# Stick-breaking attention: scores and values on the full array, tails in float32r, and one float32 group per head

## The chip, the core and the metric

The kernel runs on one core of a Trainium2 chip. The metric is the time of one execution in device microseconds; lower is better. Engine names as the profile has them: PE is TensorE (PEld its weight loads), ACT ScalarE, DVE VectorE, POOL GpSimd, SP SyncE, which issues the DMAs.

## What is computed

A decoder trunk of two layers on 256 positions of 1024 features, in float32. Each sub-layer is a norm, a modulation whose columns are products of the condition `c` with `mod_w`, a mixer or a SwiGLU, and a gated sum onto `x`. The change lies in the mixer of layer 0, which has eight gMLP heads and eight heads of stick-breaking attention:

```python
z = jnp.einsum('bqhd,bkhd->bhqk', qb, kb) * scale            # scores
before = s_pos < t_pos
log_1mb = jnp.where(before, -jax.nn.softplus(z), 0.0)
tail = lax.cumsum(log_1mb, axis=3, reverse=True) - log_1mb   # tails
w = jnp.where(before, jnp.exp(jax.nn.log_sigmoid(z) + tail), 0.0)
outs.append(jnp.einsum('bhqk,bkhd->bqhd', w.astype(v.dtype), v[:, :kv_len]))   # values
```

and around it

```python
proj = h @ w_in          # u, v of the gMLP heads; q, k, v of the attention
y_a = u * sv             # gMLP: v normed, mixed over positions ("gating")
x = x + g2[:, None, :] * (jnp.concatenate([y_a, y_b], -1) @ w_out)
```

## The kernel before

Activations are kept transposed: features on the 128 partitions, the 256 positions in the columns. A large product is made of three float32r products (`mm3`, L473): each operand is split into a rounded high half and the rest, and high x high, high x low and low x high are summed in PSUM. Weights come as 1 MB loads into four buffers (`raw`); ScalarE casts the high halves (`split_hi`, h_...), VectorE subtracts to get the low ones (`split_lo`, l_...), each 128x1024. A product of two float32 operands without a split needs no halves; its instruction runs as two passes.

Every instruction is placed by hand in one program order, and each engine keeps it. A planner, `Pace` (L36), estimates the end of every engine's work as the kernel is written out. `pump` (L453), called after blocks of products, runs what is due: splits, deferred evictions (`defer`, `run_deferred`) and the dots of the modulation columns (`mod_step`, L406). One dot is a VectorE instruction over 128x1024 (mw) that yields one eighth of a column vector; a load of mw brings two of them into one of two buffers, and the next load is issued behind the second dot. `mod_need` (L432) runs what is still missing at once. The columns (0, 7), mod07, scale the input of the SwiGLU behind the mixer: `enter` (L481) asks for them, and VectorE's updates of `xT` and the new `hh` come after that.

`hybrid` (L774) runs the mixer. q and k go into the tiles qT and kT, two heads in one 128-row block, 64 rows each. Then a loop over i = 0 to 10 (L1006) staggers the eight heads:

- `scores(h)` (L901): three float32 products of 64x128 into one bank `z`. Deferred behind it is the softplus: Abs, Exp and Ln on ScalarE into `sp`, max and sum on VectorE, and a causal mask by GpSimd (`diag`, L897, 128x256).
- `tails(h)` (L923), two rounds later: `sp` times `negtri` (384 columns) and times `neg1` (128 columns) are added onto `z`, in float32. Deferred: ScalarE's exponential into `w`, and GpSimd's mask of `w`.
- `values(h)` (L939), one more round later: three float32 products of `w` with 64 columns of `vb` into one half of the partitions of a bank `py`. Deferred for each pair of heads: the split into yh and yl.
- `fill(n)` takes n steps of other work: the projections `pvb` (products of 512 columns) and `pu` (of 256). From i = 7 on, the output projection `pdh` takes that place.
- `gating(j)` (L968), twice: sixteen float32 products of 64 columns, `pg`. `gelu_u` (L990) loads ScalarE's gelu table, runs it, and loads the old table back.

Behind the loop come the rest of the output projection, from yh and yl and from the split gMLP result (ahya, alya), and its last unit (`down_last`, L617). The next layer part starts with `pe`, whose products read hh.

```python
            if 0 <= i - 2 < 8:
                tails(i - 2)
            if i in (5, 6):
                gating(i - 5)
            if 0 <= i - 3 < 8:
                values(i - 3)
```

Of the kernel before, what the change touches and what calls it, by code (L numbers as in the profile page):

```python
# [20 lines left out]
HD = 64  # L21
# [4 lines left out]
HALF = 8  # L26
# [62 lines left out]
def trunk(ctx: ExitStack, tc: tile.TileContext, x, c, mod_w, cols,  # L89
# [124 lines left out]
    def cp(out_, in_):  # L214
        fill_act([in_], [out_])
        nc.scalar.copy(out=out_, in_=in_)  # L216
        return clk.op("act", free(out_) * 0.833 + 92, [in_], [out_])
# [14 lines left out]
    def keep_if(t, pattern, cmp, mult=-1):  # L232

        nc.gpsimd.affine_select(out=t, in_=t, pattern=pattern, base=0, channel_multiplier=mult, compare_op=cmp,
                                fill=0.0)
        return clk.op("pool", free(t) * 1.0 + 110, [t], [t])
# [21 lines left out]
    nc.vector.memset(eps_t, EPS)  # L258
    mean_w = const.tile([P, P], F32, name="mean_w")
    nc.gpsimd.memset(mean_w, 1.0 / D)  # L260
    neg1 = const.tile([P, P], F32, name="neg1")
    nc.gpsimd.memset(neg1, -1.0)
    negtri = const.tile([P, P], F32, name="negtri")
    nc.gpsimd.memset(negtri, -1.0)

    keep_if(negtri, [[-1, P]], ALU.is_ge, 1)

    cond = const.tile([P, D], F32, name="cond")

# [170 lines left out]
    def defer(t, fn):  # L440
        i = len(deferred)
        while i and deferred[i - 1][0] > t:
            i -= 1
        deferred.insert(i, (t, fn))

    def run_deferred(force=False):
        while deferred and (force or deferred[0][0] <= clk.pe):
            if state["on"] and can_l() and q["l"] - q["take"] < LOW and lo_start() <= clk.dve + SLACK:
                split_lo()
            else:  # L450
                deferred.pop(0)[1]()
# [322 lines left out]
    def hybrid(nxt):  # L774
# [31 lines left out]
        def run(gen):  # L806
            for _ in gen:
                pass

        qT = new(mix, "qT", "qT", 1, (P, 4, S))  # L810
        kT = new(mix, "kT", "kT", 1, (P, 4, S))

        def first_qk():
            for j in range(2):
                u, col = unfold(ps0[0][j], r, f"q{j}")
                ts(qT[:, j, :], u, col[:, 0:1], HD ** -0.5, ALU.add, ALU.mult)
                u, col = unfold(ps0[1][j], r, f"k{j}")
                ts(kT[:, j, :], u, col[:, 0:1], None, ALU.add)

        defer(clk.pe + 4000, first_qk)  # L820
        psq = dbank("pq1")
# [2 lines left out]
                                  scale=HD ** -0.5))  # L824
        psk = dbank("pk1")
        run(proj_t(psk, 4))
        defer(clk.pe, lambda: cp(kT[:, 2:4, :], psk.rearrange("p (j s) -> p j s", j=2)))


        wsT = new(mix, "wsT", "wsT", 1, (P, 8, P))  # L830
# [59 lines left out]
        def fill(n):  # L890
            for _ in range(n):
                next(filler, None)
# [3 lines left out]

        def diag(t):  # L897
            tv = t[:, 0:256].rearrange("p (b t) -> p b t", b=2)
            keep_if(tv, [[0, 2], [1, P]], ALU.is_gt)

        def scores(h):  # L901
            z = gbank(f"z{h}")
            r0 = 64 * (h % 2)
            qs = qT[r0:r0 + 64, h // 2, :]
            ks = kT[r0:r0 + 64, h // 2, :]
            for i, (s, t) in enumerate(((0, 0), (1, 1), (0, 1))):
                mm(z[:, i * P:(i + 1) * P], ks[:, s * P:(s + 1) * P], qs[:, t * P:(t + 1) * P], i == 0, True)
            zz = z[:, 0:384]
            sp = new(work, "e1", f"sp{h}", 4, (P, 384))

            def chain():
                act(sp, zz, AF.Abs)
                act(sp, sp, AF.Exp, scale=-1.0)
                defer(act(sp, sp, AF.Ln, bias=1.0), softplus)

            def softplus():
                stt(sp, zz, 0.0, sp, ALU.max, ALU.add)
                diag(sp)
                zs[h] = (z, sp)

            defer(clk.pe, chain)

        def tails(h):  # L923
            while h not in zs:
                run_deferred(True)
            z, sp = zs.pop(h)
            zz = z[:, 0:384]
            mm(zz, negtri, sp, False, False)
            mm(z[:, 256:384], neg1, sp[:, 128:256], False, True)
            w = new(work, "ah", f"w{h}", 4, (P, 384), F32R).bitcast(F32)  # L930

            def weights():
                act(w, zz, AF.Exp)
                diag(w)
                ws[h] = w

            defer(clk.pe, weights)

        def values(h):  # L939
            while h not in ws:  # L940
                run_deferred(True)
            w = ws.pop(h)
            hp, r0 = h // 2, 64 * (h % 2)
            if h % 2 == 0:
                pys[hp] = (dbank if hp < 2 else gbank)(f"py{hp}")
            py = pys[hp]
            for i, (s, t, src) in enumerate(((0, 0, 0), (0, 1, 2), (1, 1, 1))):
                mm(py[r0:r0 + 64, t * P:(t + 1) * P], vb[:, s, h * HD:(h + 1) * HD], w[:, src * P:(src + 1) * P],
                   i == 0, i == 2)
            if h % 2 == 1:  # L950
                if hp % 2 == 0:
                    ah = new(work, "ah", f"yh{hp}", 4, (P, 2, S), F32R)
                    al = new(work, "al", f"yl{hp}", 4, (P, 2, S), F32R)
                    yb.append((ah, al))
                ah, al = yb[-1]

                def keep():
                    defer(cp(ah[:, hp % 2, :], py[:, 0:S]), keep_lo)

                def keep_lo():  # L960
                    tt(al[:, hp % 2, :], py[:, 0:S], ah[:, hp % 2, :].bitcast(F32), ALU.subtract)

                defer(clk.pe, keep)

# [3 lines left out]
        def gating(j):  # L968
            pg = dbank(f"pg{j}")
            for i in range(2):  # L970
                hp = 2 * j + i
                for e in range(2):
                    for n in range(2):
                        h = 2 * hp + e
                        mm(pg[64 * e:64 * e + 64, i * S + n * P:i * S + (n + 1) * P], v[:, n, h * HD:(h + 1) * HD],
                           wsT[:, h, :], i == 0 and n == 0, True)

            def keep():
                for i in range(2):
                    hp = 2 * j + i  # L980
                    bb = bs_bc[:, hp, :].unsqueeze(1).to_broadcast([P, 2, P])
                    stt(yas[j][:, i, :].rearrange("p (n t) -> p n t", n=2),
                        pg[:, i * S:(i + 1) * S].rearrange("p (n t) -> p n t", n=2),
                        cols_a[:, VG + hp:VG + hp + 1], bb, ALU.mult, ALU.add)

            defer(clk.pe, keep)
# [16 lines left out]

        banks = []
        out_b = None
        for i in range(11):  # L1006
            if i < 8:
                scores(i)
            fill((3, 3, 2, 1, 2, 1, 2, 1, 1, 1, 1)[i])
            if 0 <= i - 2 < 8:  # L1010
                tails(i - 2)
            if i == 9:
                defer(clk.pe, gelu_u)
            if i in (5, 6):
                gating(i - 5)
            if i >= 7:
                if i == 7:
                    run(filler)
                    run_deferred(True)
                    banks += [dbank(f"pdh_{b}") for b in range(4)]  # L1020
                    out_b = down_steps(banks, lambda: yb[0], True)
                for _ in range(4):
                    next(out_b, None)
            if 0 <= i - 3 < 8:
                values(i - 3)
        run(out_b)
        run_deferred(True)
        down(banks, *yb[1], False)
# [360 lines left out]
```

## Time and profile before

| | |
|---|---|
| Median of three runs | 990.71 us (990.59 to 990.95) |
| The profiled execution | 990.8 us, of which the span of instructions is 989.1 |
| PE busy | 975.3 us, 99% of the span |
| PEld busy | 959.7 us, 97% |
| DVE busy | 764.0 us, 77% |
| ACT busy | 491.8 us, 50% |
| POOL busy | 24.7 us, 3% |
| Chain that ended last, by engine | PE 94%, DVE 4%, ACT 1%, DMA 1% |
| Mean granted TensorE clock | 0.996 of full speed |

Busy times of engines overlap, and a busy PE need not be at its peak. The chain is followed back from the last instruction: at each step to what released it, or to the instruction before it on its engine. The attention stage runs from about 250.7 us to 303.2 us of the span.

### The profile page before, as it was taken

To read this page: it belongs to the slowest core of one execution; us is meant where nothing else is said; L and a number is where in the kernel's file an instruction comes from. 1 tells how busy PE (TensorE), PEld (TensorE's weight loads), DVE (VectorE), ACT (ScalarE), POOL (GpSimd) and SP (SyncE) were. 2 spreads that over 40 slices of the span, in tenths; PEclk is the share of its full clock that TensorE was granted. 3 is DMA by queue.
4 is the path that set the end of the run, shared out by engine and by line. 5 is a ranking of instruction groups with operands and counts; after the bars stand their busy time and mean duration, and the time that the engine had idled before them with its cause. 6 is when DMAs were issued, how large, how long until landed. Compare 5 with 4: busy or idle time off the path is not lost.

```text
span 989.1 us, 18921 instructions
## 1 busy us (share of the span) xinstructions
PE 975.3 (99%) x7958; PEld 959.7 (97%) x7958; DVE 764.0 (77%) x1118; ACT 491.8 (50%) x691; POOL 24.7 (3%) x34
## 2 busy tenths in 40 slices
PE   6999999999999999999999999999999999999997
PEld 6999999999789999999999999999999999999997
DVE  6988877889878987777789777778998798744432
ACT  3566344365756754443466434444644574444333
POOL 4000000000220000000000000000000000000000
PEclk8999999999999999999999999999999999999999
DMA  9988997965877388897865988888269729665401
GB/s 354 331 312 286 330 335 279 332 213 188 315 253 256 130 294 298 304 324 282 294 222 164 329 320 315 294 319 298 80 210 338 254 89 322 229 214 171 170 2 43
DMA packets 144213, 249.59 MB, mean 252 GB/s; under 512 B 4216, under 2 KB 107520, under 8 KB 144128
## 3 DMA queue, kind: packets, MB, share of 16 engines
q1 hardware_dynamic: 144128, 248.39, 70.9%
q8 instruction: 62, 1.02, 0.4%
q14 instruction: 23, 0.19, 0.1%
HBM read 247.32 MB, written 1.05 MB: 251 GB/s over the span
## 4 chain that ended last, share of the span: by engine, by line
PE 94%; DVE 4%; ACT 1%; DMA 1%; issue 0%; DVEq 0%; SPq 0%; ACTq 0%
PE pf L139 44%; PE pd L139 25%; PE pc L139 3%; PE pe L139 3%; PE pcb L139 2%; PE pdc L139 2%; DVE mws L199 1%; PE pdh L139 1%; PE z L139 1%; PE pu L139 1%; PE pvb L139 1%; PE peh L139 1%; PE pec L139 1%; PE pv L139 1%; PE ps L139 1%; PE py L139 1%
## 5 line engine op out<-in xcount | busy, mean ns | idle before, releaser
L139 PE MATMUL pd<-ah,l_d 128*128 128x256 f32 x704 | 198.2, 281 | 0.0
L139 PE MATMUL pd<-al,h_d 128*128 128x256 f32 x704 | 198.0, 281 | 0.0
L139 PE MATMUL pd<-ah,h_d 128*128 128x256 f32 x704 | 198.0, 281 | 0.0
L139 PE MATMUL pf<-hh,h_u 128*128 128x256 f32 x608 | 172.0, 283 | 0.0
L139 PE MATMUL pf<-hl,h_u 128*128 128x256 f32 x608 | 171.2, 282 | 0.0
L139 PE MATMUL pf<-hh,l_g 128*128 128x256 f32 x608 | 171.1, 281 | 0.0
L139 PE MATMUL pf<-hl,h_g 128*128 128x256 f32 x608 | 171.0, 281 | 0.0
L139 PE MATMUL pf<-hh,h_g 128*128 128x256 f32 x608 | 171.0, 281 | 0.0
L139 PE MATMUL pf<-hh,l_u 128*128 128x256 f32 x608 | 170.9, 281 | 0.0
L199 DVE CUSTOM_DVE_ANT_0 mw<-mw,cond,cols_sb 128x1024 f32<-128x1024 f32 x128 | 163.7, 1306 | 3.4 <-DMA mw<-in_mod_w_dram 3.4
L216 ACT CAST h_d<-w_d 128x1024 fp32r<-128x1024 f32 x88 | 88.4, 1047 | 125.4 <-PE pf L139 98.8
L176 DVE TENSOR_TENSOR l_d<-w_d,h_d 128x1024 fp32r<-128x1024 f32 x88 | 104.5, 1221 | 55.9 <-ACT h_d L216 55.9
L216 ACT CAST h_g<-w_g 128x1024 fp32r<-128x1024 f32 x82 | 85.9, 1048 | 114.8 <-issue 78.8
L139 PEld LDWEIGHTS pd<-al,h_d 128*128 128x128 f32 x704 | 132.6, 188 | 0.0
L139 PEld LDWEIGHTS pd<-ah,h_d 128*128 128x128 f32 x704 | 132.5, 188 | 0.0
L139 PEld LDWEIGHTS pd<-ah,l_d 128*128 128x128 f32 x704 | 132.5, 188 | 0.0
L176 DVE TENSOR_TENSOR l_g<-w_g,h_g 128x1024 fp32r<-128x1024 f32 x82 | 100.0, 1220 | 40.1 <-ACT h_g L216 40.0
L139 PEld LDWEIGHTS pf<-hh,l_u 128*128 128x128 f32 x608 | 115.1, 189 | 0.0
L139 PEld LDWEIGHTS pf<-hl,h_u 128*128 128x128 f32 x608 | 114.9, 189 | 0.0
L139 PEld LDWEIGHTS pf<-hh,l_g 128*128 128x128 f32 x608 | 114.8, 189 | 0.0
L139 PEld LDWEIGHTS pf<-hh,h_g 128*128 128x128 f32 x608 | 114.8, 189 | 0.0
L139 PEld LDWEIGHTS pf<-hh,h_u 128*128 128x128 f32 x608 | 114.8, 189 | 0.0
(302 smaller groups left out, 1927.1 us busy)
## 6 DMA issues: line engine op xcount, KB each, us to landing
mw<-in_mod_w_dram SPq DMA_DIRECT2D x64, 1024.0 KB, 7.0
w_d<-in_ffn_w_down_dram SPq DMA_DIRECT2D x44, 1024.0 KB, 6.4
w_g<-in_ffn_w_gate_dram SPq DMA_DIRECT2D x41, 1024.0 KB, 6.2
w_u<-in_ffn_w_up_dram SPq DMA_DIRECT2D x41, 1024.0 KB, 5.0
mws<-in_mod_w_dram SPq DMA_DIRECT2D x14, 512.0 KB, 7.0
w_ho<-in_hy_w_out_dram SPq DMA_DIRECT2D x4, 1024.0 KB, 9.1
w_cc<-in_sc_w_in_dram SPq DMA_DIRECT2D x4, 1024.0 KB, 5.3
w_cx<-in_sc_w_in_dram SPq DMA_DIRECT2D x4, 1024.0 KB, 7.4
```

What stands on the lines that cost most here:

```text
L139: return nc.tensor.matmul(out=out_, lhsT=lhsT, rhs=rhs, start=start, stop=stop, skip_group_check=True)
L176: nc.vector.tensor_tensor(out=out_, in0=a, in1=b, op=op)
L199: nc.vector.tensor_tensor_reduce(out=src, in0=src, in1=cond, scale=scale, scalar=init, op0=ALU.mult, op1=ALU.add, accum_out=dst)
L216: nc.scalar.copy(out=out_, in_=in_)
```

## The change

Five things. The scores use all 128 rows: k is kept in two versions, in each of which the 64 rows of the other head of the pair are zero (memsets by GpSimd; the second version of the heads 4 to 7 and of the heads 0 to 3 lies in the tiles of `al`). The values use all 128 columns: the product takes both heads of a pair from `vb`, each head of the pair has a half of the bank's columns, and the half of the rows that belongs to it is read out, so the evictions into kT, yh and yl are done in two instructions of 64 partitions. The tails take float32r products of the softplus split into `sh` (ScalarE cast, behind the mask) and `sl` (VectorE subtraction); `negtri` and `neg1` become float32r. `w` takes the place of `sp`. And the loop is written in another order: a part of the fill, values, gating, scores, the rest of the fill, tails.

```diff
+        kT1 = [new(work, "al", f"kT1{k}", 4, (P, 2, S), F32R).bitcast(F32) for k in range(2)]
+        kTs = [[kT[:, 2 * k:2 * k + 2, :] for k in range(2)], kT1]
+        heads = [slice(64 * e, 64 * e + 64) for e in range(2)]
+        for e in range(2):
+            for k in range(2):
+                zeros = kTs[e][k][heads[1 - e]]
+                nc.gpsimd.memset(zeros, 0.0)
...
-            qs = qT[r0:r0 + 64, h // 2, :]
-            ks = kT[r0:r0 + 64, h // 2, :]
+            qs = qT[:, h // 2, :]
+            ks = kTs[h % 2][h // 4][:, h // 2 % 2, :]
...
-                diag(sp)
-                zs[h] = (z, sp)
+                defer(diag(sp), halves)
+
+            def halves():
+                sh = new(work, "sq", f"sh{h}", 2, (P, 384), F32R)
+
+                def rest():
+                    sl = new(work, "sl", f"sl{h}", 2, (P, 384), F32R)
+                    tt(sl, sp, sh.bitcast(F32), ALU.subtract)
+                    zs[h] = (z, sp, sh, sl)
+
+                defer(cp(sh, sp), rest)
...
-            mm(zz, negtri, sp, False, False)
-            mm(z[:, 256:384], neg1, sp[:, 128:256], False, True)
-            w = new(work, "ah", f"w{h}", 4, (P, 384), F32R).bitcast(F32)
+            for part in (sh, sl):
+                mm(zz, negtri, part, False, False)
+                mm(z[:, 256:384], neg1, part[:, 128:256], False, part is sl)
+            w = sp
...
-                mm(py[r0:r0 + 64, t * P:(t + 1) * P], vb[:, s, h * HD:(h + 1) * HD], w[:, src * P:(src + 1) * P],
+                mm(py[:, c0 + t * P:c0 + (t + 1) * P], vb[:, s, hp * P:(hp + 1) * P], w[:, src * P:(src + 1) * P],
...
+        def beside(n):
+            if out_b is None:
+                fill(n)
+            else:
+                for _ in range(3 * n):
+                    next(out_b, None)
+
         for i in range(11):
+            if i == 8:
+                run(filler)
+                run_deferred(True)
+                banks += [dbank(f"pdh_{b}") for b in range(4)]
+                out_b = down_steps(banks, lambda: yb[0], True)
+            beside((0, 0, 1, 1, 1, 1, 1, 1, 2, 2, 2)[i])
+            if 0 <= i - 3 < 8:
+                values(i - 3)
+            if i in (5, 6):
+                gating(i - 5)
             if i < 8:
                 scores(i)
-            fill((3, 3, 2, 1, 2, 1, 2, 1, 1, 1, 1)[i])
+            if i == 9:
+                defer(clk.pe, gelu_u)
+            beside((3, 3, 1, 1, 1, 1, 0, 0, 0, 0, 0)[i])
             if 0 <= i - 2 < 8:
                 tails(i - 2)
```

TensorE's row at i = 6, before:

```order
L139 MATMUL z_3086<-sp_3090,negtri 128x384
L139 MATMUL z_3086<-sp_3090,neg_102 128x128
L139 MATMUL pg_3240<-wsT,v 64x128 x8
L139 MATMUL py_3184<-w_3174,vb 64x128 x3
L139 MATMUL z_3252<-qT,kT 128x128 x3
L139 MATMUL pu_3193<-hh_2443,h_uu_1_3001 128x256
```

and in the changed kernel (twelve products `pu` stand ahead of the first row, and the tails of this head's predecessor ahead of those):

```order
L139 MATMUL pu_3183<-hh_2445,l_uu_1_3064 128x256
L139 MATMUL py_3205<-sp_3090,vb 128x128 x3
L139 MATMUL pg_3275<-wsT,v 64x128 x8
L139 MATMUL z_3284<-qT,kT 128x128 x3
L139 MATMUL z_3147<-sh_3201,negtri 128x384
L139 MATMUL z_3147<-sh_3201,neg_102 128x128
L139 MATMUL z_3147<-sl_3229,negtri 128x384
L139 MATMUL z_3147<-sl_3229,neg_102 128x128
L139 MATMUL pu_3183<-hh_2445,h_uu_1_3011 128x256
```

The tails moved from ahead of the values to behind the scores, and only a fill stands between the tails of a head and its values.

ScalarE's row at the last two heads (w6 and w7 are the exponentials before; in the changed kernel they are written onto sp6 and sp7), before:

```order
L211 ACTIVATE w6_3333<-z6_3188 128x384
L216 CAST h_ho1_1_3348<-w_ho1_3031 128x1024
L216 CAST yh2_3357<-py2_3327 128x256
L211 ACTIVATE w7_3361<-z7_3252 128x384
L226 ACT_TABLE_LOAD
L211 ACTIVATE uT_2836<-uT_2836 128x1024
L226 ACT_TABLE_LOAD
```

and in the changed kernel:

```order
L216 CAST yh2_3384<-py2_3324 64x256 x2
L211 ACTIVATE sp6_3288<-z6_3284 128x384
L216 CAST h_ho1_1_3403<-w_ho1_3072 128x1024
L226 ACT_TABLE_LOAD
L211 ACTIVATE uT_2844<-uT_2844 128x1024
L226 ACT_TABLE_LOAD
L211 ACTIVATE sp7_3332<-z7_3328 128x384
```

The exponential of the last head moved behind the gelu and its two table loads.

VectorE's row at the end of the mixer, from the last low half that both kernels have there to the first update of `xT`, before:

```order
L176 TENSOR_TENSOR l_g01_1_1_3545<-w_g01_1_3274,h_g01_1_1_3513 128x1024
L199 ISA mw072_3298,mod07_3282<-mw072_3298,cond_107,cols_sb_89 128x1024
L199 ISA mod07_3282 128x1
L199 ISA mw073_3352,mod07_3282<-mw073_3352,cond_107,cols_sb_89 128x1024
L199 ISA mod07_3282 128x1
L199 ISA mw073_3352,mod07_3282<-mw073_3352,cond_107,cols_sb_89 128x1024
L199 ISA mod07_3282 128x1
```

and in the changed kernel, where one dot of mw070 already stands ahead of the first row:

```order
L176 TENSOR_TENSOR l_g01_1_1_3596<-w_g01_1_3312,h_g01_1_1_3562 128x1024
L199 ISA mw070_3356,mod07_3580<-mw070_3356,cond_109,cols_sb_89 128x1024
L199 ISA mod07_3580 128x1
L199 ISA mw071_3418,mod07_3580<-mw071_3418,cond_109,cols_sb_89 128x1024
L199 ISA mod07_3580 128x1
L199 ISA mw071_3418,mod07_3580<-mw071_3418,cond_109,cols_sb_89 128x1024
L199 ISA mod07_3580 128x1
L176 TENSOR_TENSOR l_u01_1_1_3607<-w_u01_1_3455,h_u01_1_1_3594 128x1024
L199 ISA mw072_3601,mod07_3580<-mw072_3601,cond_109,cols_sb_89 128x1024
L199 ISA mod07_3580 128x1
L199 ISA mw072_3601,mod07_3580<-mw072_3601,cond_109,cols_sb_89 128x1024
L199 ISA mod07_3580 128x1
```

Two more dots, of mw073, follow. SyncE's row of loads at the same place, before:

```order
L391 DMA mw072_3298<-in_mod_w_dram 128x2x1024
L391 DMA mw073_3352<-in_mod_w_dram 128x2x1024
L301 DMA w_u01_1_3383<-in_ffn_w_up_dram 128x8x256
L301 DMA w_g01_2_3491<-in_ffn_w_gate_dram 128x8x256
L301 DMA w_u01_2_3511<-in_ffn_w_up_dram 128x8x256
L301 DMA w_d01_0_3547<-in_ffn_w_down_dram 128x2x1024
L391 DMA mw080_3550<-in_mod_w_dram 128x2x1024
```

and in the changed kernel:

```order
L393 DMA mw071_3418<-in_mod_w_dram 128x2x1024
L303 DMA w_u01_1_3455<-in_ffn_w_up_dram 128x8x256
L303 DMA w_g01_2_3526<-in_ffn_w_gate_dram 128x8x256
L303 DMA w_u01_2_3544<-in_ffn_w_up_dram 128x8x256
L303 DMA w_d01_0_3598<-in_ffn_w_down_dram 128x2x1024
L393 DMA mw072_3601<-in_mod_w_dram 128x2x1024
L393 DMA mw073_3605<-in_mod_w_dram 128x2x1024
```

The loads mw072 and mw073 moved from ahead of w_u01_1 to behind w_d01_0.

## Rows read from the trace of the kernel before

**Rows 1.** Waits of TensorE: waiting and releaser, us in total, times, longest.

```profile
PE ps L139 <- ACT hh L216: 4.6, 1, 4.6
```

**Rows 2.** Chain in order of time, the stage: start, us, engine, tile, line, instructions.

```profile
233.91 5.70 PE pk L139 x48
239.61 11.13 PE pv L139 x48
...
268.42 0.87 PE z L139 x4
...
302.39 0.80 PE py L139 x6
```

**Rows 3.** The same chain at the end of the mixer.

```profile
311.85 1.06 ACT h_g L216
...
314.16 1.26 DVE mw L199
```

**Rows 4.** Instructions in time, TensorE: start, us from first start to last end.

```profile
250.35 0.40 PE L139 MATMUL pv<-h_v,hl 128*128 128x512 f32 x1
250.67 0.93 PE L139 MATMUL z<-qT,kT 64*128 64x128 f32 x6
251.53 0.50 PE L139 MATMUL pvb<-h_vb,hh 128*128 128x512 f32 x1
251.87 0.39 PE L139 MATMUL pvb<-l_vb,hh 128*128 128x512 f32 x1
...
268.25 0.81 PE L139 MATMUL z<-sp,negtri 128*128 128x384 f32 x2
268.90 0.38 PE L139 MATMUL z<-sp,neg 128*128 128x128 f32 x2
269.21 0.87 PE L139 MATMUL py<-w,vb 128*64 128x128 f32 x6
...
320.32 0.28 PE L139 MATMUL pe<-hh,h_g 128*128 128x258 f32 x1
```

**Rows 5.** Instructions on tile z: count, ns least/median/most, first and last start.

```profile
L139 PE MATMUL z<-sp,neg x16: 271/274/275, 265.6 to 298.3; 128*128 128x128 f32 x16
```

**Rows 6.** Instructions in time, ScalarE.

```profile
269.32 0.49 ACT L211 ACTIVATE w<-z 128x384 f32<-128x384 f32 x1
...
295.74 1.04 ACT L216 CAST h_ho<-w_ho 128x1024 fp32r<-128x1024 f32 x1
...
299.43 1.28 ACT L226 ACT_TABLE_LOAD   x1
...
303.10 0.62 ACT L216 CAST ahya<-ya 128x512 fp32r<-128x512 f32 x1
```

**Rows 7.** Instructions in time, GpSimd; in brackets the idle time ahead.

```profile
269.10 1.39 POOL L234 TENSOR_SCALAR_AFFINE_SELECT sp<-sp 128x256 f32<-128x256 f32 x1 [2.04 <-DVE sp L187]
```

**Rows 8.** Instructions on tile sp, the masks: ns least/median/most.

```profile
L234 POOL TENSOR_SCALAR_AFFINE_SELECT sp<-sp x8: 406/837/1448, 259.6 to 290.4; 128x256 f32<-128x256 f32 x8
```

**Rows 9.** Instructions in time, VectorE.

```profile
268.95 1.27 DVE L199 CUSTOM_DVE_ANT_0 mw<-mw,cond,cols_sb 128x1024 f32<-128x1024 f32 x1
...
305.49 1.23 DVE L176 TENSOR_TENSOR l_g<-w_g,h_g 128x1024 fp32r<-128x1024 f32 x1
306.63 1.22 DVE L176 TENSOR_TENSOR l_u<-w_u,h_u 128x1024 fp32r<-128x1024 f32 x1
...
317.87 0.17 DVE L176 TENSOR_TENSOR hl<-mod,hh 128x16 fp32r<-128x16 f32 x1
```

**Rows 10.** Loads of mw issued from 291 to 296.5 us, issue to landing.

```profile
DMA to landing us min/median/max: 4.7/4.8/5.0
```

**Rows 11.** Loads of mw issued from 314 to 320 us, behind other loads.

```profile
DMA to landing us min/median/max: 8.2/8.2/8.2
```

**Rows 12.** Two stretches, TensorE: bounds, us, busy (instructions), granted clock, DMA.

```profile
20.46:25.35 4.89, 4.28 (x18) 0.50 1.04 421
303.12:320.32 17.20, 17.20 (x146) 1.00 0.67 239
```

More of the change, by code (lines that the diff above doesn't have):

```diff
@@ L260, in trunk @@
     nc.gpsimd.memset(mean_w, 1.0 / D)
[L261 to L266, printed above, removed]
+    neg1 = const.tile([P, P], F32R, name="neg1")
+    negtri = const.tile([P, P], F32R, name="negtri")
+    minus = new(lop, "lo", "minus", HALF, (P, 1024), F32R).bitcast(F32)[:, 0:P]
+    nc.gpsimd.memset(minus, -1.0)
+    nc.gpsimd.tensor_copy(out=neg1, in_=minus)
+    keep_if(minus, [[-1, P]], ALU.is_ge, 1)
+    nc.gpsimd.tensor_copy(out=negtri, in_=minus)
     cond = const.tile([P, D], F32, name="cond")
@@ L811, in hybrid @@
         kT = new(mix, "kT", "kT", 1, (P, 4, S))
+        kT1 = [new(work, "al", f"kT1{k}", 4, (P, 2, S), F32R).bitcast(F32) for k in range(2)]
[5 more added lines that the diff above has]
+                nc.gpsimd.memset(zeros, 0.0)
+                clk.op("pool", 600.0, [], [zeros])
         def first_qk():
@@ L817, in first_qk @@
                 u, col = unfold(ps0[1][j], r, f"k{j}")
-                ts(kT[:, j, :], u, col[:, 0:1], None, ALU.add)
+                for e in range(2):
+                    ts(kTs[e][0][heads[e], j, :], u[heads[e]], col[heads[e], 0:1], None, ALU.add)
         defer(clk.pe + 4000, first_qk)
@@ L826, in hybrid, with second_k @@
         run(proj_t(psk, 4))
-        defer(clk.pe, lambda: cp(kT[:, 2:4, :], psk.rearrange("p (j s) -> p j s", j=2)))
+        def second_k():
+            for e in range(2):
+                cp(kTs[e][1][heads[e]], psk[heads[e]].rearrange("p (j s) -> p j s", j=2))
+        defer(clk.pe, second_k)
         wsT = new(mix, "wsT", "wsT", 1, (P, 8, P))
@@ L898, in diag @@
             tv = t[:, 0:256].rearrange("p (b t) -> p b t", b=2)
-            keep_if(tv, [[0, 2], [1, P]], ALU.is_gt)
+            return keep_if(tv, [[0, 2], [1, P]], ALU.is_gt)
         def scores(h):
             z = gbank(f"z{h}")
-            r0 = 64 * (h % 2)
-            qs = qT[r0:r0 + 64, h // 2, :]
-            ks = kT[r0:r0 + 64, h // 2, :]
+            qs = qT[:, h // 2, :]
+            ks = kTs[h % 2][h // 4][:, h // 2 % 2, :]
             for i, (s, t) in enumerate(((0, 0), (1, 1), (0, 1))):
@@ L925, in tails @@
                 run_deferred(True)
-            z, sp = zs.pop(h)
+            z, sp, sh, sl = zs.pop(h)
             zz = z[:, 0:384]
-            mm(zz, negtri, sp, False, False)
-            mm(z[:, 256:384], neg1, sp[:, 128:256], False, True)
-            w = new(work, "ah", f"w{h}", 4, (P, 384), F32R).bitcast(F32)
+            for part in (sh, sl):
+                mm(zz, negtri, part, False, False)
+                mm(z[:, 256:384], neg1, part[:, 128:256], False, part is sl)
+            w = sp
             def weights():
@@ L942, in values @@
             w = ws.pop(h)
-            hp, r0 = h // 2, 64 * (h % 2)
+            hp, c0 = h // 2, S * (h % 2)
             if h % 2 == 0:
@@ L957, in keep @@
                 def keep():
-                    defer(cp(ah[:, hp % 2, :], py[:, 0:S]), keep_lo)
+                    for e in range(2):
+                        t_h = cp(ah[heads[e], hp % 2, :], py[heads[e], e * S:(e + 1) * S])
+                    defer(t_h, keep_lo)
                 def keep_lo():
-                    tt(al[:, hp % 2, :], py[:, 0:S], ah[:, hp % 2, :].bitcast(F32), ALU.subtract)
+                    for e in range(2):
+                        tt(al[heads[e], hp % 2, :], py[heads[e], e * S:(e + 1) * S],
+                           ah[heads[e], hp % 2, :].bitcast(F32), ALU.subtract)
                 defer(clk.pe, keep)
@@ L1005, in hybrid @@
         out_b = None
-        for i in range(11):
+        def beside(n):
[4 more added lines that the diff above has]
+                    next(out_b, None)
+        for i in range(11):
+            if i == 8:
[8 more added lines that the diff above has]
+                gating(i - 5)
             if i < 8:
                 scores(i)
-            fill((3, 3, 2, 1, 2, 1, 2, 1, 1, 1, 1)[i])
+            if i == 9:
+                defer(clk.pe, gelu_u)
+            beside((3, 3, 1, 1, 1, 1, 0, 0, 0, 0, 0)[i])
             if 0 <= i - 2 < 8:
                 tails(i - 2)
[L1012 to L1025, printed above, removed]
         run(out_b)
```

## Prediction, made before the changed kernel ran

> **What bounds the kernel now.** I read four views. First TensorE's waits: the longest is 4.6 us at the kernel's start, and none lies in the attention stage or behind it [rows 1]. Until the last output TensorE is the bound, and a microsecond taken from its row is a microsecond gained as long as nothing else comes late. Second, the chain in order of time: every step of the stage, up to the last values at 303.19 us, is TensorE's [rows 2]. Third, what stands just behind TensorE at the end of the layer. There the chain leaves TensorE at 311.85 and goes over ScalarE's split half and VectorE's dots of the modulation columns (mw) [rows 3], while TensorE is busy until 320.32: both arrive together, and the columns have no slack. Fourth, what single products cost.
>
> **Prices of products.** Forty-eight float32r products of 256 columns take 5.70 us, of 512 columns 11.13: 0.119 and 0.232 us each [rows 2]. A float32 product runs as two passes. Two passes of 128 columns at full shape span 0.38 us [rows 4] and one lasts 0.274 [rows 5], so one starts 0.11 behind the other; two of 384 columns take 0.65 (268.25 to 268.90), 0.32 each [rows 4].
>
> **Term 1, geometry.** The scores use 64 rows of the array, the values 64 columns; their neighbours use 128x128. Six passes of scores should take 6 x 0.11 = 0.66 us, but the next product starts 0.86 behind (250.67 to 251.53). The scores start 0.32 after their forerunner where 0.232 is usual, and the second product behind them follows by 0.34 [rows 4]. That is 0.20 + 0.09 + 0.11 = 0.39 us for two switches of shape. The tails, float32 at full shape, follow float32r products without such a step, so I lay it to the shape and not to the type. There are 28 switches: four scores stand alone among full products (8), two stand behind values and two behind gating and values (3 switches each, 12), four values stand alone (8). 28 x 0.195 = 5.5 us; entering the 64-column values costs 0.06 less (a group of 0.87 where scores have 0.93 [rows 4]), six times, and gating overlaps some of its own, so I take 4.9. Afterwards only the two gating groups are left at half size: 4 switches, 0.7. The passes at full shape cost 0.11 as before. Gain 4.2 us, 3.5 to 4.9.
>
> **Term 2, tails.** Before, per head, 2 x 0.32 + 2 x 0.11 = 0.87 us, as the chain has it [rows 2]. After, two float32r products of 384 columns, half way between 0.119 and 0.232, so 0.175 each, and two of 128. No row has a float32r product of 128 columns: from above it is bounded by float32's 0.22 for both passes, from below by the line through 256 and 512 columns, 0.06. I take 0.11, the least distance of products that each bring their own weights in rows 4. So 2 x 0.175 + 2 x 0.11 = 0.57, a gain of 0.30 x 8 = 2.35 us; the bounds are 0.6 and 3.1. The Trainium skill (TensorE: Matmul & The Clock Gate, Back-to-back issue gap) gives N/2.4 + 2.5 ns, by an estimate 0.056 us for 128 columns, which would make this gain 3.2 us; its section on LDWEIGHTS counts 128 weight columns at 0.107 us, and the 0.11 of the trace is nearer to that.
>
> **Term 3, a new wait before the values.** Before, another head's scores, tails and a fill stood between the tails of a head and its values. Now only a fill is left: 12 products (1.43 us) for heads 0 to 4, 18 (2.14) for 5 to 7, plus 0.11 of the tails' own. In that time the last tails product drains in 0.274 [rows 5], ScalarE's exponential takes 0.49 [rows 6], GpSimd's mask 0.41 at best [rows 8], three hand-overs some 0.05 each and the first weights 0.1: 1.42 of 1.54 us, if nobody is in the way. But a mask took 1.39 from 269.10 on, where VectorE ran a dot from 268.95 on [rows 7, 9], 0.98 more, and half-splits of 1.04 [rows 6] stand ahead of exponentials in ScalarE's row. I count 1.0 per head for heads 0 to 4 (one of the two obstacles, now and then both), 0.25 for heads 5 and 6 (more cover). Head 7 has a half-split, both table loads and the gelu ahead of its exponential; the last three took 3.67 us (299.43 to 303.10) [rows 6]. From the tails of head 6 to values 7 the row of ScalarE so adds up to some 6.5 us, TensorE's to 5.9, and the small casts yh come on top: 1.5. Sum 5 + 0.5 + 1.5 = 7.0 us; low end 3.5 (0.5 in five heads, 1 in the last), high end 10. The Trainium skill (GPSIMD Engine Reference, Key points) says that GpSimd shares its SBUF interfaces with VectorE and names instructions with two SBUF inputs; the trace agrees with 1.39 against 0.41 us. The new halves sh and sl, a ScalarE cast and a VectorE subtraction like those of the chain, lie two rounds ahead of their tails and are hidden there; without that cover they would add a microsecond per head at the tails.
>
> **Term 4, the columns come last.** By the order, the planner puts the dots off when VectorE is fuller. Before, five of the eight dots of mod07 are done in the stage, and three are left behind the half-split l_g01_1_1. After, all eight stand behind the stage, and SyncE issues mw072 and mw073 behind w_d01_0. I count from E, the end of the last values, 303.12 before; from there TensorE has 17.20 us of products [rows 12] and no more. VectorE's first half-split starts at E + 2.0 (before 2.37, behind casts that now run earlier), and they come every 1.14 us [rows 9]. Six are through at 8.8, a dot (1.26 [rows 3]) at 10.1, the seventh half-split at 11.2, three dots at 12.5, 13.8 and 15.0. A load of mw needs one of two buffers that dots set free: mw072 goes out at 12.6, mw073 at 15.1. In the same place before, a mw load behind w_g, w_u and w_d took 8.2 us to land [rows 11]. So mw072 lands at 20.8, its two dots end at 23.4, those of mw073 at 25.9. From the last dot to the first product of the next layer it was 320.32 - 317.87 = 2.45 us [rows 4, 9]: E + 28.4 against 17.2 of work, a wait of 11.2 us. With the 4.7 to 5.0 us that lone loads took [rows 10] it is 8. I take 11.
>
> **Term 5, the clock.** After the early pause of 4.6 us [rows 1] the granted clock was 0.50, that is 1.2 GHz, for the 4.89 us in which TensorE then ran 18 products [rows 12]. At that level the time per product is nearly twice that of 2.4 GHz: 2.2 us lost, of which some 0.4 would be waiting anyway. I take 1.75 for the pause of term 4; bounds 0.9 and 3.5.
>
> **Sum.** Against the profiled execution, 990.8 us (span 989.1; the median of the runs, 990.71, is the same): 990.8 - 4.2 - 2.35 + 7.0 + 11.0 + 1.75 = 1004.0 us. GpSimd's zero fills of kT and the casts of kT and y in two parts are short work on engines with idle time there; I cost them at nothing. Nothing behind the layer gives the loss back, since TensorE does not wait there now [rows 1].
>
> **Rivals.** (a) The values wait little, because ScalarE and GpSimd happen to be free: term 3 is 2, the columns stay late, 999. Against it: half of the softplus masks now last 0.84 us or more [rows 8]. (b) The columns are in time and only the values wait: 990.8 - 6.55 + 7 = 991.2, no change. (c) Faster: VectorE gets ahead in TensorE's waits, the eighth dot ends by E + 14.75 (where the last of three ends now), and the waits are at their low end: 990.8 - 6.55 + 3.5 = 987.8. Against (b) and (c): seven half-splits and eight dots are 18 us of VectorE by themselves, and all of them stand behind the cast of the last values. (d) The change doesn't do what it says: the switch hangs on the type and stays, or 128 columns of float32r cost as much as float32: 1005.7 to 1008. Against the first: the tails.
>
> **Chances.** Forecast 0.68 (its own range 1001 to 1008), (a) 0.15, (b) 0.07, (c) 0.05, (d) 0.05. About 0.2% is what a measurement of this kernel can tell from no change. Slower: 0.68 + 0.15 + 0.05 = 0.88; same 0.07; faster 0.05. The range 998.5 to 1008.5 takes in the forecast, (a) and (d).
>
> **What would show it.** In the profile after: scores and values at 128*128 with 0.66 us per group and neighbours at 0.232 and 0.119 (term 1); the four tails products in 0.57 us (term 2); TensorE waiting for GpSimd before py, about 7 us in eight times (term 3); one wait of about 11 us before the next layer's first product, with VectorE's dots and two late loads in the chain (term 4); a clock of 0.5 right behind it (term 5). The forecast is wrong if TensorE does not wait there, or if mw073 lands before the layer's last product.

## The result, and the profile after

The changed kernel takes 1006.0 us (median of four runs, 1005.13 to 1006.90) against 990.66 of the kernel before in the same comparison: a ratio of 1.015, 95% interval 1.0138 to 1.0163. It is 15.3 us slower, where 13.3 (to 1004.0) were forecast; the range was 998.5 to 1008.5. The profiled execution has a span of 1005.2 us, 16.1 more than before.

TensorE's waits, in the form of [rows 1] (waiting and releaser, us in total, times, longest). First the matmuls:

```profile
PE pe L139 <- ACT hh L221: 10.6, 1, 10.6
PE py L139 <- POOL sp L234: 5.6, 7, 1.8
```

and the weight loads, on which the wait of a product sits first:

```profile
PEld py L139 <- POOL sp L234: 7.2, 8, 2.0
```

Two waits are new: eight times before the values (py), and once before the next layer's first product (pe). Both were forecast, at 7.0 us and at 11.

The products themselves became cheaper. The chain in order of time in the stage (start, us, engine, tile, line, instructions):

```profile
250.72 0.67 PE z L139 x6
251.39 4.17 PE pvb L139 x18
...
263.87 0.53 PE z L139 x4
```

The scores of a head take 0.67 us, where the next product stood 0.86 behind them in [rows 4]; the four tails products take 0.53 where [rows 2] have 0.87. Only around the gating, which is left at half size, do scores still cost 0.88:

```profile
278.16 0.94 PE py L139 x6
279.10 1.08 PE pg L139 x16
280.18 0.88 PE z L139 x6
```

The tails one by one, TensorE in time (start, us from start to end):

```profile
263.70 0.34 PE L139 MATMUL z<-sh,negtri 128*128 128x384 f32 x1
263.88 0.22 PE L139 MATMUL z<-sh,neg 128*128 128x128 f32 x1
263.94 0.39 PE L139 MATMUL z<-sl,negtri 128*128 128x384 f32 x1
264.17 0.22 PE L139 MATMUL z<-sl,neg 128*128 128x128 f32 x1
264.22 0.33 PE L139 MATMUL pu<-hh,h_uu 128*128 128x256 f32 x1
```

From start to start these are 0.18, 0.06, 0.23 and 0.05 us: 0.52 in all.

How a wait before the values comes about, in the chain of head 1:

```profile
269.54 0.57 DVE sp L187
270.10 0.06 issue
270.16 0.72 POOL sp L234
270.88 0.57 issue
271.45 0.41 POOL sp L234
271.86 0.04 issue
271.90 0.95 PE py L139 x6
```

Two masks stand in a row in GpSimd. The one at 270.16 is the softplus mask of a later head; only the second, 0.41 us long, is the mask of w1 that the values need. The first lasts until 271.45, since VectorE runs a half-subtraction beside it. Over the stage the masks last (tile sp; ns least, median, most):

```profile
L234 POOL TENSOR_SCALAR_AFFINE_SELECT sp<-sp x16: 401/712/1389, 258.0 to 303.2; 128x256 f32<-128x256 f32 x16
```

The end of the mixer on VectorE (in brackets the idle time ahead of the instruction and what ended it):

```profile
306.45 1.23 DVE L176 TENSOR_TENSOR l_g<-w_g,h_g 128x1024 fp32r<-128x1024 f32 x1 [0.22 <-ACT h_g L216]
...
309.93 1.23 DVE L176 TENSOR_TENSOR l_g<-w_g,h_g 128x1024 fp32r<-128x1024 f32 x1 [1.11 <-ACT h_g L216]
...
325.16 1.34 DVE L199 CUSTOM_DVE_ANT_0 mw<-mw,cond,cols_sb 128x1024 f32<-128x1024 f32 x1 [3.27 <-DMA mw<-in_mod_w_dram]
...
329.06 1.34 DVE L199 CUSTOM_DVE_ANT_0 mw<-mw,cond,cols_sb 128x1024 f32<-128x1024 f32 x1 [1.28 <-DMA mw<-in_mod_w_dram]
...
331.59 0.17 DVE L176 TENSOR_TENSOR hl<-mod,hh 128x16 fp32r<-128x16 f32 x1
```

The end of the last values, E, is taken as in the prediction (303.12 there): it is the start of the first product behind them, here 304.31 us. The first half-subtraction is at E + 2.1, four dots of mod07 follow the next low halves, the last of them from 319.41 on, and VectorE then waits 3.27 us for mw072 and 1.28 for mw073, and the columns are there at E + 27.3. The two late loads, issue to landing (stretches 318 to 319 and 320.5 to 321.5 us):

```profile
mw<-in_mod_w_dram SPq DMA_DIRECT2D x1, 1024.0 KB, 6.8
```

```profile
mw<-in_mod_w_dram SPq DMA_DIRECT2D x1, 1024.0 KB, 8.1
```

And the clock, stretches of TensorE (bounds, us, busy and instructions of PE, PEld, DVE, ACT and POOL, granted clock, DMA share, GB/s):

```profile
305.07:308.48 3.41, 3.41 (x18) 3.41 (x17) 2.87 (x4) 2.26 (x3) 0.00 (x0) 0.50 0.86 303
...
333.78:339.20 5.42, 5.42 (x24) 5.18 (x24) 5.39 (x13) 4.80 (x10) 0.00 (x0) 0.50 0.96 363
339.20:348.54 9.34, 9.34 (x78) 9.29 (x78) 6.31 (x17) 5.42 (x11) 0.00 (x0) 1.00 0.00 0
```

Behind the pause the granted clock is 0.50, 1.2 GHz, until 339.20, as forecast. A second such stretch, 305.07 to 308.48, follows the wait for the last head's weights; it was not in the sum.

### The profile page after: what moved, and what is told of

It reads as the page before. It is cut to its first block, busy times and chain, and to the rows that moved or that the text cites. A ratio compares the mean times of both kernels' runs of the same rounds, so it can differ in the third digit from the quotient of the medians.

```text
span 1005.2 us, 18963 instructions
## 1 busy us (share of the span) xinstructions
PE 976.2 (97%) x7958; PEld 964.5 (96%) x7958; DVE 771.0 (77%) x1132; ACT 497.1 (49%) x704; POOL 28.3 (3%) x39
## 4 chain that ended last, share of the span: by engine, by line
PE 88%; DVE 3%; DMA 3%; ACT 2%; issue 1%; POOL 1%; SPq 0%; POOLq 0%; DVEq 0%; ACTq 0%
PE pf L139 43%; PE pd L139 25%; PE pe L139 4%; PE pc L139 3%; PE pcb L139 2%; PE pdc L139 2%; DMA w_s<-in_ffn_w_up_dram 1%; PE pec L139 1%; PE peh L139 1%; PE pvb L139 1%; PE pv L139 1%; DVE mws L199 1%; POOL sp L234 1%; DMA mws<-in_mod_w_dram 1%; DMA mw<-in_mod_w_dram 1%
```

## Experiments

The change has four parts that can be made one by one: geometry, tails, loop, and, not written as such in it, how many dots the planner places in the stage. "Theory A" below is that of the prediction: the loop makes the values wait for GpSimd's mask, and a fuller VectorE makes the planner put dots off, so that the columns are late. The stretches in this table are worked out from starts in TensorE's row: first scores to E (the start of the first product behind the last values), E to the first pe, and that to the first pf. The median and the difference are those of the run and of before on the same chip.

| kernel | scores to E | E to pe | pe to pf | median, us | difference | ratio, 95% |
|---|---|---|---|---|---|---|
| before | 52.44 | 17.20 | 12.46 | | | |
| after | 53.75 | 29.47 | 14.60 | 1006.0 | +15.3 | 1.0138 to 1.0163 |
| e1 geometry | 48.54 | 25.86 | 14.46 | 997.57 | +5.4 | 1.0048 to 1.0078 |
| e2 tails | 50.38 | 23.68 | 14.56 | 998.87 | +6.7 | 1.0059 to 1.0089 |
| e3 loop | 58.47 | 17.19 | 11.93 | 997.11 | +5.0 | 1.0042 to 1.0072 |
| e4 geometry and tails | 47.90 | 28.45 | 14.57 | 1000.44 | +8.3 | 1.0074 to 1.0108 |
| e5 geometry, dots placed | 48.55 | 17.60 | 12.60 | 988.62 | -2.3 | 0.9964 to 0.9984 |
| e6 tails, dots placed | 50.38 | 17.20 | 12.45 | 989.80 | -1.1 | 0.9978 to 0.9996 |
| e7 after, dots placed | 59.05 | 17.17 | 12.05 | 997.41 | +6.5 | 1.0051 to 1.0082 |
| e8 both, old loop, dots placed | 46.75 | 17.47 | 12.83 | 986.75 | -4.1 | 0.9945 to 0.9970 |
| e9 after, no mask of w | 49.03 | 27.74 | 14.39 | 1001.16 | +9.9 | 1.0086 to 1.0120 |
| e10 after, pause filled | 53.84 | 28.96 | 12.83 | 1004.49 | +13.2 | 1.0116 to 1.0146 |
| e11 after, no table loads | 52.88 | 29.35 | 14.10 | 1005.40 | +14.2 | 1.0126 to 1.0156 |

The stretches of one kernel and another are compared to a tenth of a microsecond; differences of medians are not that good (last section), so a difference of under 1.5 us between two rows of the last columns is not read.

### e1 to e3: one part at a time

e1 takes from the change's diff only the parts on kT, scores, values and the evictions behind them; e2 only the types of negtri and neg1, sh and sl, the tails and w; e3 only the new loop.

> The kernel before with the geometry alone: scores and values at full size; float32 tails and the old loop stay. Theory A (planner): the products give back some 4 us (scores 0.86 to 0.66 us per head, neighbours at 0.232 and 0.119), values hardly wait, but the casts in two parts fill VectorE, the planner puts dots off, and by the order five of the eight dots of mod07 stand behind the last low half: the next layer waits some 7.6 us, and at half the clock behind it loses 1.5 to 2 more. 990.7 - 4 + 7.6 + 1.7 = 996. Theory B (the new loop is to blame for late columns): no wait there, 986.5.

> The kernel before with the float32r tails alone (halves sh and sl, w in the place of sp); half-size scores and values and the old loop stay. Theory A: tails give 0.3 us per head, 2.5 in all; the eight subtractions sl fill VectorE, by the order six of the eight dots stand behind the stage: a wait of some 6.7 us before the next layer and 1.7 for the clock. 990.7 - 2.5 + 6.7 + 1.7 = 996.6. Theory B: 988.2.

> The kernel before with the new loop alone: half-size scores and values, float32 tails. Theory A: TensorE waits for w before the values of most heads, 5 to 7 us in all, and since that time lets dots run in the stage (by the order two of eight stand behind it), the next layer waits little: 990.7 + 5.5 = 996, and at most one short stretch of half clock. Theory B: the values wait and the columns come late as in the changed kernel, 1006 to 1012.

Measured: each part alone makes the kernel slower, by 5.4, 6.7 and 5.0 us. TensorE's waits in e1, e2 and e3, one row for each:

```profile
PE pe L139 <- ACT hh L221: 8.3, 1, 8.3
```

```profile
PE pe L139 <- ACT hh L221: 6.3, 1, 6.3
```

```profile
PE py L139 <- POOL w L234: 5.8, 5, 1.4
```

e1 and e2 have no wait before the values to speak of, and in the stage they gain 3.9 and 2.1 us; all of that and more goes in the one wait for the columns. e3 has no wait for the columns, and its stage is 6.0 us longer, although its products are those of before. So Theory B (the new loop is to blame for the late columns) is wrong, and Theory A's division holds: the loop makes the waits for GpSimd, geometry and tails make the columns late, each of them by itself. The size of e1's wait stands out. The planner prices a product by its columns and its type (`mm`), and e1 leaves both as they were. So what put off dots is something that looks like nothing: the casts of kT and y in two parts, the zero fills, or the buffers that kT1 takes. No run takes these three apart. In its trace five of the eight dots of mod07 start behind the stage, two of them as late as 321.36 and 322.63 us, where the kernel before had three left.

### e4: geometry and tails in the old loop

> The changed kernel with the loop of before: full-size scores and values and float32r tails. Theory A: the values wait under 1 us in all, the products give 6.5 us, but all eight dots stand behind the stage and the next layer waits 10 to 11 us, with about 2 for the clock: 990.7 - 6.5 + 1 + 10.6 + 2 = 998. So of the 15.3 us lost the loop accounts for some 8, the dots for the rest. Theory B: no waits of either kind, 984.2.

Measured: +8.3 us, and the stage 4.5 us shorter than before. The wait for the columns is 10.7 us as in the changed kernel. Taking the new loop away so gives back 7 of the 15.3 us; the 8.3 that stay are what the late columns cost, less the 4.5 gained in the stage. Theory A said +7.3.

### e5 and e6: the same parts, dots placed by hand

```diff
         for i in range(11):
+            while mq["step"] < (32, 34, 35, 35, 35, 37, 39, 40, 42, 44, 44)[i]:
+                mod_step()
...
+        while mq["step"] < 45:
+            mod_step()
         run(out_b)
```

> The kernel before with the geometry alone, and the dots of the modulation columns forced at the places of the loop where the kernel before has them (32, 34, 35, 35, 35, 37, 39, 40, 42, 44, 44 and 45 done). Theory A (the loss of e1 is only that the planner put dots off): no wait before the next layer and no stretch of half clock there; what is left is the gain of the stage in e1, 3.9 us: 990.7 - 3.9 = 986.8. Theory C (VectorE has no room for the dots in the stage): the forced dots push the softplus back, tails or values wait, and the time is at 990 or above.

> The kernel before with the float32r tails alone, dots forced at the places of before. Theory A: the wait of e2 goes, the gain of the stage in e2, 2.1 us with one wait of 0.5 for vb in it, stays: 990.7 - 2.1 = 988.6. Theory C: the eight subtractions sl leave VectorE no room, tails wait, 990 or above.

Measured: 2.3 and 1.1 us faster than before. In both traces TensorE waits no more before pe, E to pe is 17.60 and 17.20 us, and the gain of the stage is the same as in e1 and e2: 3.89 and 2.06 us. That is Theory A in the traces; the medians show 1.6 and 1.0 us less than these gains (see the last point of the document). Theory C (VectorE has no room) is wrong for the old loop. The columns were late because of where the dots were put, not because the engine could not have done them.

### e7: the changed kernel, dots placed by hand

The same lines in the new loop.

> The changed kernel with the dots forced at the places of before. Theory A, additive: the wait of 10.6 us before the next layer and the half clock behind it (2.1) go, the waits before the values stay: 1006 - 12.7 = 993.3. Theory C: five more dots in the stage are 6.3 us of VectorE in the one place where values already wait for the chain of the softplus and for GpSimd beside VectorE; the values wait 2 to 5 us more: 995 to 998. Less than 2 us gained would mean that the dots are not the cause.

Measured: +6.5 us against before, where additive losses would have left some +2.6; E to pe is 17.17 us. The values wait longer instead, and that is Theory C:

```profile
PE py L139 <- POOL sp L234: 9.4, 7, 3.6
```

The chain ahead of the longest of these waits:

```profile
276.48 0.58 DVE mw L199
277.06 0.63 issue
277.69 0.08 DVE mod L199
277.77 1.20 DVE mw L199
...
279.01 0.57 DVE sp L187
...
279.71 1.62 POOL sp L234 x2
281.33 0.04 issue
281.38 1.51 PE py L139 x6
```

Two dots stand ahead of a softplus step on VectorE, the softplus mask follows that, and the mask of w follows the softplus mask. The products' waits grow so from 5.6 to 9.4 us. The stage is 5.3 us longer than in the changed kernel; most of the rest is a low clock behind this longest wait (0.53 on average from 281.38 to 284.90), at which values and gating take some 1.5 us more. In the new loop there is no place for the dots that does not cost: put off they make the next layer wait, put in they make the values wait. With e5 and e6 this says that the loop, with one fill between tails and values, is what takes the room away.

### e8: the parts that gain, in the old loop

As e4, with other places of the dots and the gelu one round earlier:

```diff
+            while mq["step"] < (32, 34, 35, 35, 36, 38, 40, 41, 43, 44, 44)[i]:
+                mod_step()
...
-            if i == 9:
+            if i == 8:
                 defer(clk.pe, gelu_u)
```

> The changed kernel with the loop of before, dots forced (32, 34, 35, 35, 36, 38, 40, 41, 43, 44, 44 done) and the gelu one round earlier, so that its table loads are through before the last exponential. Theory A: both losses are gone and the gains of e5 and e6 add up, less small waits: 990.7 - 5.6 = 985, faster than both kernels. Theory C: 989 to 992.

Measured: 986.75 us, 4.1 faster than before and 19 faster than the change. The stage is 5.69 us shorter, and this is the one wait of a product that the view lists from the attention on:

```profile
PE py L139 <- ACT vb L216: 0.4, 1, 0.4
```

Of the whole change the geometry and the float32r tails are gains. The loop and the planner's answer turned them into a loss. What the earlier gelu has of the 4.1 us was not measured by itself; in e4, where it stands as before, the output projection waited 0.7 us for uT.

### e9: the changed kernel without the mask of w

```diff
-                act(w, zz, AF.Exp)
-                diag(w)
+                act(w, zz, AF.Abs)
+                clk.op("pool", 366.0, [w], [w])
```

The second line only tells the planner the same time, so that the order stays.

> The changed kernel without GpSimd's mask of w; the exponential behind which it stands is an absolute value of the same size, so the weights are not those of the reference. The order of all else stays. Theory A (the mask, slow beside VectorE, is what the values wait for, and the columns' chain is counted from the last values): the waits before the values fall from 7 us to 2 or less, the last values end some 5 us earlier, the wait before the next layer stays at 10 to 11, and the short half clock behind the last values goes: 1006 - 5 - 1.3 = 999.7. Theory D (the end is set by dots and loads, whatever the values do): the values come earlier, the next layer waits 5 us more: 1005. Theory E (ScalarE's row is what the values wait for): the waits fall by 2 us at most: 1004.

Measured: the last values end 4.7 us earlier than in the changed kernel (49.03 against 53.75 behind the first scores), pe starts 6.45 us earlier by the same count, and the median stands at +9.9 instead of +15.3. Waits:

```profile
PE pe L139 <- ACT hh L221: 10.4, 1, 10.4
PE py L139 <- ACT sp L211: 2.4, 2, 2.2
```

So some 4.7 of the 7 us before the values are GpSimd's mask and what it queues behind; what is left is ScalarE's, nearly all of it (2.2) at the last head, behind the gelu and its tables. Theory D (the end is set by dots and loads whatever the values do) is wrong, Theory E too. That pe gains 1.7 us more than E has its cause mostly in the row of 309.93 above: there VectorE idled 1.11 us for a cast h_g, which by the chain waited for TensorE's products (4.26 us for 23 of them, most of them at the low clock). The other half microsecond is mw073, which landed after 7.6 us instead of 8.1. In e9 no stretch of low clock follows the last values, and the same half-subtractions follow each other without a gap:

```profile
302.60 1.22 DVE L176 TENSOR_TENSOR l_u<-w_u,h_u 128x1024 fp32r<-128x1024 f32 x1
303.74 1.22 DVE L176 TENSOR_TENSOR l_g<-w_g,h_g 128x1024 fp32r<-128x1024 f32 x1
```

### e10: the pause filled

```diff
         down_last(banks, *split_a[1], mod_cols[(0, 5)], hi, lo)
+        pbusy = gbank("pbusy")
+        for _ in range(92):
+            nc.tensor.transpose(out=pbusy[:, 0:P], in_=ident, identity=ident)
```

> The changed kernel with 92 transposes of the identity, 0.109 us each as in the start's warm-up, behind the last product of the mixer: 10.0 us of work for TensorE in a wait of 10.9. Theory A (the pause is what lowers the clock): the granted clock stays at 1.0 behind it, the next 98 products take 12.6 us as before the change instead of 14.8: 1006 - 2.1 = 1003.9. If the pause isn't the cause, the clock is 0.5 again and the time stays at 1006; if the transposes run past the end of the wait, it grows.

Measured: 2.1 us less than the change (+13.2 against +15.3), as expected. The pause and what follows it:

```profile
322.90:333.00 10.10, 10.10 (x94) 9.96 (x92) 7.00 (x14) 1.08 (x3) 0.00 (x0) 1.00 0.78 262
333.00:346.00 13.00, 12.74 (x101) 12.29 (x101) 11.09 (x27) 9.88 (x19) 0.00 (x0) 1.00 0.41 153
```

With TensorE at work the granted clock stays at 1.00, 2.4 GHz, and pe to pf takes 12.83 us instead of 14.60. The idle pause is the cause of the low clock.

### e11: no table loads around the gelu

```diff
-            table("gelu_and_others")
-            act(uT, uT, AF.Gelu)
+            clk.act += 1285.0
+            act(uT, uT, AF.Abs)
```

and the load behind it alike.

> The changed kernel without the two table loads around the gelu (which is an absolute value here, so the output is not the reference's): ScalarE's row ahead of the last exponential is 2.56 us shorter. Theory A: the wait before the last values, 2.0 us, falls to 0.6 or less, the stretch of half clock behind it (3.4 us of the trace, 1.3 lost) goes too, and the columns' chain follows the last values: 1006 - 1.4 - 1.3 = 1003.3. Theory D: 1005 to 1006.

Measured: +14.2 us, 1.2 less than the change where Theory A said 2.7 less; a difference as small as 1.2 is not read. In the trace two of its three steps came as expected. From the last pdh product ahead of them to the last values it is 0.6 us instead of 2.1, and behind them the clock is full:

```profile
304.63:308.50 3.87, 3.87 (x35) 3.87 (x34) 3.60 (x6) 3.83 (x7) 0.00 (x0) 1.00 1.00 384
```

The third did not: TensorE is done sooner and then waits longer, 12.0 us instead of 10.6.

```profile
PE pe L139 <- ACT hh L221: 12.0, 1, 12.0
```

E is 0.87 us earlier behind the first scores (head 0 waited 0.6 us longer in this trace), pe 1.0. The half-subtractions run without a gap here too, and mw072 is issued at E + 13.4 instead of 13.9, but its load took longer than the 6.8 us of the changed kernel:

```profile
318.04 8.54 DMA mw<-in_mod_w_dram
```

So the full clock is worth little to the products up to pe, which lie under the wait for the columns; what it could give to the columns, the load took. How much of the 1.7 us it would be with equal loads stays open.

## Why the prediction was right, and where it was off

The mechanism was right in every step that decides: TensorE's new waits are those before the values and before the next layer, and no others. By its terms, against the profiled execution:

- **Geometry (said -4.2):** e1 and e5 measure 3.9 us less in the stage, within the 3.5 to 4.9 given. That scores and values lose their step while their types stay float32 speaks against the rival that it hangs on the type.
- **Tails (said -2.35):** 0.52 us per head instead of 0.87, so 2.8 for eight heads; e2 has 2.1 with one wait of 0.5 for vb in it. The 0.11 for a product of 128 columns was the wrong end: from start to start it is 0.06, the lower bound. But the product of 384 columns behind it takes 0.23, 0.05 more than the first, so that the four come to little less than the 0.57 of the sum.
- **Values (said +7.0):** 7.2 us on the weight loads, eight times. The cause is right (e9), the way it goes is not in every head: I reckoned with a mask of w that VectorE slows, 1.0 for each of the heads 0 to 4. So it is in head 0. In heads 1 to 3 the slowed one is the softplus mask of a later head, and a fast mask of w stands behind it in GpSimd's row. In head 4 the mask of w was fast and nothing stood ahead of it: its wait of 0.6 us is for the exponential, which ScalarE came to late. So the sum is right in part by luck. The order of the masks was there to be read.
- **Columns (said +11.0):** E to pe grew by 12.3 us, most of it one wait of 10.6. Two loads behind w_d01_0, four dots ahead of them, 2.2 us from the last dot to pe: as said. The mis-sized step is the row of half-subtractions, reckoned at 1.14 us each: the third waited 1.11 for its cast, the dot that should end at E + 15.0 ended at 16.4, and pe came at E + 29.5 instead of 28.4. The cast had waited for TensorE at the low clock. One thing came out right by luck: mw072 was issued 1.3 us later than reckoned, landed in 6.8 us instead of 8.2, and so was there at E + 20.8 as said.
- **Clock (said +1.75):** 2.1 us behind the pause, from pe to pf, confirmed by e10. The other stretch of low clock was not foreseen: the rule by which term 5 was made, a pause and then half the clock, was applied to the long wait alone and not to the wait before the last values. Nor would it have been a safe rule there: in e9 a wait of 2.2 us at the same place was followed by the full clock.

First scores to E is 1.3 us longer (0.45 in the sum), E to pe 12.3 (11.0), pe to pf 2.1 (1.75), and 0.4 lie in the rest: 16.1 of span against 13.2.

One sentence of the prediction is wrong though its sum is right: the zero fills and the casts in two parts, "short work on engines with idle time there", were costed at nothing. e1 has them and the full-size products alone, and loses 8.3 us at the columns. The sum did not suffer, because term 4 was read from the order of the whole change, which had the dots already put off. And what the prediction could not say is how the parts hang together. Its terms stood side by side as if they added up; e7 shows that they don't, since the dots taken from the end come back as waits before the values.

## What to carry to other kernels

A saving on the engine that bounds a kernel is only worth what the others leave of it: here 5.7 us saved on TensorE moved the end by 4.1, and only after five dots of another engine had been put back by hand. Where a planner's estimates set the order, look after each edit, the small ones too, at what it moved far away, and where a load and its consumer now stand. And a round of other work between a product and its use is a buffer against every slow instruction in the chain between them; before cutting it down, count what is queued ahead of each step of that chain, on each engine.

## What the runs showed of the hardware

- **A product of 128 columns in float32r is 0.06 us from start to start, and the next one pays.** 384 columns take 0.18 us behind a long product and 0.23 behind a short one. The Trainium skill (TensorE: Matmul & The Clock Gate, Back-to-back issue gap) gives, by an estimate from its formula for a single product, 0.056 us, and says that in a stream the weight loads set the spacing too. The trace agrees with the first; the 0.05 that the next product takes longer would fit the second, but no run shows that the weight load is the reason.
- **GpSimd's mask beside VectorE.** The mask takes 0.41 us alone. In [rows 7, 9] a dot runs from 268.95 to 270.22, and the mask that starts at 269.10 ends at 270.49, 0.27 behind it; after the change the slowed masks end 0.26 or 0.27 behind a half-subtraction or dot that was running when they began, too. Where VectorE's instruction began behind the mask, the mask kept to 0.41. So it did at 290.17 and 294.47, beside a softplus step of VectorE that was running already and that reads z from PSUM. No run varied this by itself. The Trainium skill (GPSIMD Engine Reference, Key points) tells of shared SBUF interfaces; that it matters which of the two began first, and which instruction VectorE runs, is from the traces.
- **A wait in the stage can bring the low clock, and need not.** In the changed kernel, after 1.8 us of waiting until 303.62, TensorE had a clock of 0.50 for 3.41 us from 305.07 on; after the 10.6 us before pe for 5.42. With work in the pause it stayed at 1.00 (e10). In e7 a wait of 3.6 us was followed by the low clock too. In e3, which waits five times, 5.8 us in all and 1.4 at most, the clock stayed at 1.00 through the stage. And in e9 TensorE waited 2.2 us before the last values, longer than in the changed kernel, and behind them the clock was full:

```profile
299.33:316.40 17.07, 17.07 (x147) 17.07 (x145) 16.12 (x20) 9.05 (x12) 0.00 (x0) 1.00 0.87 301
```

So neither the length of one wait nor the sum of a stage's waits (5.6 us in the changed kernel) settles it; what does stays open.
- **The start of the kernel varies.** The first product behind the early pause starts at 20.14 us in e10 and at 21.63 in e11, with nothing changed ahead of it:

```profile
20.14 0.58 PE L139 MATMUL ps<-hh,h_s 128*128 128x256 f32 x1 [4.64 <-ACT hh L216]
```

```profile
21.63 0.58 PE L139 MATMUL ps<-hh,h_s 128*128 128x256 f32 x1 [4.64 <-ACT hh L216]
```

All later times move with it: the first scores start at 250.20 and 251.75. Over the thirteen traces the first number is 19.98 to 21.63, about the spread of the runs of one kernel (before: 990.31 to 992.05 beside e5 to e8). The difference arises in the eight products of the first norm (pr_start, at about 11 us): they start 0.40 to 0.43 us apart in e11, and 0.22 apart from the second on in e10, so that ScalarE's first step behind them (y_start) comes at 14.40 and 12.92. The profile shows a clock of 1.00 there in both, so what halves the pace stays open.
- **What the medians of e5, e6 and e8 lack.** They show 1.6, 1.0 and 1.6 us less than the gains of their stages. By the table 0.5, 0 and 0.6 of this are lost again between E and pf. Another 0.2, 0.7 and 0.2 lie outside the span of the instructions: the time of a run less its span is 1.72 us for before (median) and 1.95, 2.41 and 1.96 for these three. The 0.9, 0.3 and 0.7 us that are left are less than what the start varies by.
